# A two-layer encoder step on one core: the down-projection of the two middle feed-forwards by seven products with accumulation by DMA, other weights split in halves, six double places instead of five

## The chip, the cores and the metric

The kernel runs on one core of a Trainium2 chip. The metric is the device time of one execution in microseconds (us). Three executions of the kernel before took 2642.04, 2642.61 and 2645.54 us; the median is 2642.61 us. Everything read from a profile comes from one more execution, which took 2645.79 us.

## What is computed

A step of a hybrid encoder for 640 tokens (512 of a new stream and 8 times 16 of running streams) of width 1024. There are six sub-layers: feed-forward 0, mixer 0, feed-forward 1, feed-forward 2, mixer 1, feed-forward 3. The four feed-forwards are alike; cut to what matters:

```python
D_MODEL, D_FF = 1024, 2816

def swiglu(x, w_gate, w_up, w_down):
    return (jax.nn.silu(x @ w_gate) * (x @ w_up)) @ w_down

# around every feed-forward
x = layer_norm(ALPHA * x + 0.5 * swiglu(x, w_gate, w_up, w_down), g, b)
```

All arrays are float32. The change touches the last product, h @ w_down with h of 640 x 2816, in feed-forwards 1 and 2.

## The kernel before, in words

**Precision.** A product of float32 arrays is made of three matmuls. `split` (L92) writes a rounded high part with a cast on ScalarE (L93) and the rest, the low part, with a subtraction on VectorE (L94). A product then adds high x high, low x high and high x low in one PSUM bank. Every weight thus passes through ScalarE and VectorE before TensorE can use it: a DMA on SyncE's queue brings 128 x 1024 numbers to a `raw` place (four of them), and `split2` (L105) writes them as high and low parts to a double place `w` (a pool of `PAIRS` = 5, L29 and L46). A half, 128 x 512, goes to the single place `w1`.

**A feed-forward** (`ffn`) works through 22 blocks of 128 hidden channels. Blocks 0 and 1 are done plainly; the others in pairs f, f+1 by `pair` (L382). A pair needs two matrices, gate and up, and each of them is computed by the seven products of a 2 x 2 scheme in the place of eight. `operands` (L318) loads two weight blocks and prepares four operands: `u`, split from the raw weights, serves products 1 and 2; `v`, split from two sums, serves products 6 and 5; `w`, split from two differences, serves 7 and 3; the single `w1` serves 4. The two sums stand in the tile `sw` (L336, one buffer), s1 = a21 + a22 and s2 = s1 - a11, and are read again by the differences. `matrix` (L357) runs the products in the order 1, 2, 6, 5, 7, 3, 4, each of 12 matmuls with 320 columns, in three PSUM banks; it copies intermediate results to `mx` (ScalarE) and adds them to the results as they become ready (`take`). The gate's results pass through Silu, the up's are multiplied by it in `hf`, a float32 row of 640 tokens (two buffers), and `finish` (L243) splits that row to the high and low parts `h`.

**The down-projection** (`down`, L423) follows after four blocks: it loads four blocks of `w_down` and, for each of the five token tiles t and the two column halves j, adds 12 matmuls with 512 columns in a bank (`tm_proj`, L199), which VectorE scales and adds to the accumulator `yacc` (L206). That is 120 matmuls. It stands between the gate and the up matrix of the next group's first pair. A group of four blocks is so: gate, down of the group before, up, gate, up. Each feed-forward has five groups; the last one is projected at its end, together with the layer norm.

**Order.** A scheduler sets the order of the instructions of each engine when the program is built. On the chip each engine runs its list in that order and waits where an operand or a buffer is not ready.

Of the kernel before, what the change touches and what calls it, by code (L numbers as in the profile page):

```python
# [17 lines left out]
ALPHA = 4.0 ** 0.25  # L18
# [3 lines left out]
T = 640  # L22
TP = 512
NT = 5
KT = 8
NF = 22
HALVES = ((0, 256), (256, 384))
RAWS = 4
PAIRS = 5  # L29
PHASES = ("ffn0", "mix0", "ffn1", "ffn2", "mix1", "ffn3")  # L30
LN_OF = {"ffn0": 0, "mix0": 1, "ffn1": 2, "ffn2": 3, "mix1": 4, "ffn3": 5}

# [2 lines left out]
def kernel(ctx: ExitStack, tc: tile.TileContext, I, O, phases=PHASES):  # L35
    nc = tc.nc

    def pool(name, bufs=1, stack=ctx, **kw):
        return stack.enter_context(tc.tile_pool(name=name, bufs=bufs, **kw))
# [5 lines left out]

    pools = {"raw": pool("raw", RAWS), "w": pool("w", PAIRS), "w1": pool("w1", 1)}  # L46

# [28 lines left out]
    state = {"silu": None, "preload": None}  # L76
# [15 lines left out]
    def split(hi, lo, src):  # L92
        nc.scalar.copy(hi, src)  # L93
        return nc.vector.tensor_tensor(lo, src, hi.bitcast(F32), op=ALU.subtract)  # L94

    def raw_tile():
        return pools["raw"].tile([128, 1024], F32, name="raw")
# [4 lines left out]
    def two_units():  # L102
        return pools["w"].tile([128, 2, 2, 512], F32R, name="w")

    def split2(w, src):  # L105

        return split(w[:, :, 0], w[:, :, 1], src.rearrange("p (j c) -> p j c", j=2))

    def load_w(src):

        r = raw_tile()
        nc.sync.dma_start(r, src)
        w = two_units()
        split2(w, r)
        return w[:, 0], w[:, 1]

    def w_k(w, k):
# [8 lines left out]
    def mm3(ps, lhs, rhs):  # L126
        n = 3 * len(lhs)
        k = 0
        for (wh, wl), (xh, xl) in zip(lhs, rhs):
            for a, b in ((wh, xh), (wl, xh), (wh, xl)):  # L130
                state["pe"] = nc.tensor.matmul(ps, a, b, start=(k == 0), stop=(k == n - 1)).ins  # L131
                k += 1
# [3 lines left out]
    yacc = act.tile([128, NT, D], F32, name="yacc")  # L136
# [72 lines left out]
    def ffn(i, ph, last, side=None):  # L209


        V = nc.vector
        Q = T // 2
        with ExitStack() as st:
            wk = pool(f"ffn{i}_wk", 1, st, reuse_waits="tile")
            steps = side(wk) if side is not None else iter(())

            def tick(where):

                if ph == "ffn0" and where in range(NT):  # L220
# [40 lines left out]
            for h in range(2):  # L261
                o, L = HALVES[h]
# [86 lines left out]
            def product(ps, A, p, first):  # L349
                n = 0  # L350
                for k in range(4):
                    for a, b in ((0, 0), (1, 0), (0, 1)):
                        nc.tensor.matmul(ps, A[p][:, a, k * 128:k * 128 + 128], B[p][b][:, k, :],  # L353
                                         start=(first and n == 0), stop=(n == 11), skip_group_check=True)
                        n += 1

            def matrix(A, take):  # L357

                x, w, z = (bank_a()[:, :Q] for _ in range(3))
                e = {}  # L360

                def keep(n, ps):
                    e[n] = wk.tile([128, Q], F32, name="mx", bufs=3)
                    nc.scalar.copy(e[n], ps)  # L364


# [12 lines left out]
                product(x, A, 4, False)  # L379
                take(1, 0, x, None)  # L380

            def pair(f, before=None):  # L382
                g = first if f == 2 else {}

                def gate(r, c, ps, e):
                    if r not in g:
                        g[r] = g_row()
                    t = g[r][:, Q * c:Q * c + Q]
                    if e is not None:
                        V.tensor_tensor(t, ps, e, op=ALU.add)  # L390
                        ps = t
                    state["silu"] = nc.scalar.activation(t, ps, AF.Silu).ins

                def up(r, c, ps, e):
                    c = slice(Q * c, Q * c + Q)
                    t = row(f + r)
                    if e is not None:
                        V.tensor_tensor(t[:, c], ps, e, op=ALU.add)
                        ps = t[:, c]
                    if r == 0:  # L400
                        if c.start:
                            V.tensor_tensor(t, t, g[0], op=ALU.mult)
                            finish(f)
                    else:
                        V.tensor_tensor(t[:, c], ps, g[1][:, c], op=ALU.mult)
                        if not c.start:
                            finish(f + 1)

                for n, take in (("w_gate", gate), ("w_up", up)):
                    if n == "w_gate" and f == 2:  # L410
                        tick("gate")
                        continue
                    if n == "w_up" and before is not None:
                        down(before)
                    with tc.issue_after(state["acc0"]) if f == 2 else ExitStack():
                        A = operands(I[n][i, f], I[n][i, f + 1])
                    if n == "w_up":
                        for r in range(2):
                            ht[f + r] = h_tile()
                    matrix(A, take)  # L420
                    tick("gate" if n == "w_gate" else "up")

            def down(fs, norm=None):  # L423
                for f in fs:
                    wd[f] = load_w(I["w_down"][i, f])
                if norm is not None:
                    g_bc = [wk.tile([128, 2, 4, Q], F32, name=f"T{n}", bufs=1).rearrange("p a k c -> p (a k c)")[:, :D]
                            for n in (1, 2)]
                    load_gb(norm, g_bc)
                for t in range(NT):  # L430
                    tm_proj(t, [ht[f] for f in fs], [wd[f] for f in fs], 0.5 / ALPHA)
                    if t == 0 and fs[0] == 0:
                        state["acc0"] = state["acc"]
                        with tc.issue_after(state["acc"]):
                            t3_split()
# [1135 lines left out]
```

## Time and profile before

| what | number |
|---|---|
| median of three runs | 2642.61 us (2642.04 to 2645.54) |
| profiled execution | 2645.79 us |
| its span, first to last instruction | 2644.1 us |
| granted TensorE clock, mean over the span | 0.987 |
| busy: PE, VectorE (DVE), ScalarE (ACT), GpSimd (POOL) | 2559.6, 1914.1, 1118.3, 248.8 us |
| matmuls with 512 columns in the down-projections, of all four feed-forwards | 2640 |
| splits of a weight on DVE and of `sw` on DVE | 423 and 76 |
| HBM traffic over the span | 113 GB/s |

The profile names the engines PE (matmuls), PEld (weight loads, beside PE), DVE, ACT, POOL, and SPq for the DMAs that SyncE issues. A row of instructions says the line of the code, the engine, the operation and output <- inputs; then how many, the busy time and the mean duration of one, and the idle time of the engine before them with what ended it. Matmuls overlap one another: the mean duration of one is longer than the distance between two, so the distance is taken from the busy time of the group or from start times. Feed-forward 1 lies from about 780 to 1180 us, feed-forward 2 from there to about 1570 us.

### The profile page before, as it was taken

How to read it: one execution, taken by the hardware profiler on the slowest of the kernel's cores; microseconds unless marked ns; L12 is line 12 of the kernel's file. 1: busy time of each engine (PE TensorE's matmuls, PEld its weight loads, DVE VectorE, ACT ScalarE, POOL GpSimd, SP SyncE). 2: the span in 40 equal slices, each digit the busy share in tenths (PEclk: the TensorE clock that was granted, in tenths of full speed). 3: DMA queues.
4: the chain of work that ended last, by engine and by line, in shares of the span. 5: the costliest groups of instructions: out<-in, count | busy, mean ns of one | idle time of the engine just before them, and what ended most of it. 6: DMA issues, size and time to landing. Idle time of an engine off the chain costs nothing. (4 is left out here: it accounts for less than half of the span.)

```text
span 2644.1 us, 40071 instructions
## 1 busy us (share of the span) xinstructions
PE 2559.6 (97%) x15673; PEld 2315.7 (88%) x15673; DVE 1914.1 (72%) x3380; ACT 1118.3 (42%) x2050; POOL 248.8 (9%) x356
## 2 busy tenths in 40 slices
PE   8999999999879999999999999999999999999998
PEld 8999999887559999999999999988888878998887
DVE  7787777667858677657866567777675689876668
ACT  4433444346524344333433334566554444442332
POOL 0000002110021000003000002311121141000001
PEclk9999999999979999999999999999999999999999
DMA  5232334542312223222122223466463622443442
GB/s 178 96 99 88 103 109 144 181 144 77 93 44 71 81 96 96 70 82 98 64 76 85 87 80 106 124 183 208 123 199 111 230 90 86 159 141 109 139 129 98
DMA packets 165742, 302.72 MB, mean 114 GB/s; under 512 B 19072, under 2 KB 89856, under 8 KB 165040
## 3 DMA queue, kind: packets, MB, share of 16 engines
q1 hardware_dynamic: 163792, 293.83, 34.5%
q0 software_dynamic: 1760, 6.33, 0.7%
q8 instruction: 123, 2.02, 0.3%
q14 instruction: 67, 0.55, 0.1%
HBM read 259.56 MB, written 40.54 MB: 113 GB/s over the span
## 5 line engine op out<-in xcount | busy, mean ns | idle before, releaser
L131 PE MATMUL bank<-w,h 128*128 128x512 f32 x2640 | 612.1, 392 | 2.3 <-DVE w L94 2.3
L131 PEld LDWEIGHTS bank<-w,h 128*128 128x128 f32 x2640 | 493.5, 188 | 107.9 <-issue 3.4
L131 PE MATMUL bank<-xhi,w 128*128 128x256 f32 (+2 forms) x2528 | 560.7, 313 | 20.3 <-ACT w L93 14.2
L94 DVE TENSOR_TENSOR w<-raw,w 128x1024 fp32r<-128x1024 f32 (+1 forms) x423 | 476.4, 1136 | 121.5 <-ACT w L93 120.1
L353 PE MATMUL bank<-xhi,w 128*128 128x320 f32 x2432 | 539.6, 310 | 0.0
L93 ACT CAST w<-raw 128x1024 fp32r<-128x1024 f32 (+1 forms) x423 | 401.5, 970 | 180.0 <-DVE raw L332 81.6
L131 PEld LDWEIGHTS bank<-xhi,w 128*128 128x128 f32 x2528 | 424.0, 189 | 35.3 <-ACT w L93 15.6
L353 PE MATMUL bank<-T,w 128*128 128x320 f32 x2736 | 427.9, 310 | 3.5 <-ACT w L93 2.6
L353 PEld LDWEIGHTS bank<-T,w 128*128 128x128 f32 x2736 | 408.1, 188 | 5.3 <-ACT w L93 2.8
L353 PEld LDWEIGHTS bank<-xhi,w 128*128 128x128 f32 x2432 | 406.6, 188 | 5.5 <-issue 3.9
L131 PE MATMUL bank<-xlo,w 128*128 128x256 f32 (+2 forms) x1264 | 391.9, 311 | 1.2 <-DVE xlo L94 1.2
L353 PE MATMUL bank<-xlo,w 128*128 128x320 f32 x1216 | 375.5, 309 | 0.0
L206 DVE SCALAR_TENSOR_TENSOR yacc<-bank,yacc 128x512 f32<-128x512 f32 x240 | 164.8, 688 | 222.5 <-PE bank L131 222.4
L93 ACT CAST w<-sw 128x1024 fp32r<-128x1024 f32 x76 | 79.8, 1050 | 399.1 <-PE bank L131 270.3
L131 PEld LDWEIGHTS bank<-xlo,w 128*128 128x128 f32 x1264 | 239.5, 190 | 3.5 <-DVE xlo L94 1.7
L353 PEld LDWEIGHTS bank<-xlo,w 128*128 128x128 f32 x1216 | 228.2, 188 | 0.5 <-issue 0.5
L364 ACT COPY mx<-bank 128x320 f32<-128x320 f32 x228 | 96.6, 423 | 174.7 <-PE bank L353 174.2
L94 DVE TENSOR_TENSOR w<-sw,w 128x1024 fp32r<-128x1024 f32 x76 | 93.0, 1224 | 62.2 <-ACT w L93 61.8
L155 POOL DMA_DIRECT2D T<-in_ln_gb_dram x8 | 4.5, 568 | 1204.7 <-PE bank L353 796.5
L131 PE MATMUL bank<-w,og 128*128 128x512 f32 x432 | 106.6, 399 | 2.5 <-ACT og L1364 2.0
L131 PEld LDWEIGHTS bank<-w,og 128*128 128x128 f32 x432 | 81.0, 191 | 20.8 <-DVE og L1365 2.7
L1141 DVE SCALAR_TENSOR_TENSOR acc<-ext,cw,acc 128x512 f32<-128x512 f32 (+1 forms) x144 | 68.9, 546 | 29.8 <-POOL cvo L1131 16.7
(398 smaller groups left out, 2826.5 us busy)
## 6 DMA issues: line engine op xcount, KB each, us to landing
raw<-in_w_gate_dram SPq DMA_DIRECT2D x88, 512.0 KB, 4.1
raw<-in_w_up_dram SPq DMA_DIRECT2D x88, 512.0 KB, 4.3
raw<-in_w_down_dram SPq DMA_DIRECT2D x88, 512.0 KB, 4.1
raw<-in_m_in_dram SPq DMA_DIRECT2D x52, 512.0 KB, 4.3
raw<-in_m_out_dram SPq DMA_DIRECT2D x24, 512.0 KB, 4.1
csb<-cs_d SPq DMA_DIRECT2D x20, 512.0 KB, 5.5
h<-in_ssd_h_dram SPq DMA_DIRECT2D x16, 512.0 KB, 6.2
h<-in_ssd_h_dram SPq DMA_DIRECT2D x32, 256.0 KB, 2.8
```

The source lines that it names most:

```text
L93: nc.scalar.copy(hi, src)
L94: return nc.vector.tensor_tensor(lo, src, hi.bitcast(F32), op=ALU.subtract)
L131: state["pe"] = nc.tensor.matmul(ps, a, b, start=(k == 0), stop=(k == n - 1)).ins
L155: nc.gpsimd.dma_start(g_bc[j], bass.AP(tensor=I["ln_gb"].tensor, offset=I["ln_gb"].offset + (2 * n + j) * D, ap=[[0, 128], [1, D]]))
L206: state["acc"] = nc.vector.scalar_tensor_tensor(ya, pb, scale, ya, op0=ALU.mult, op1=ALU.add).ins
L353: nc.tensor.matmul(ps, A[p][:, a, k * 128:k * 128 + 128], B[p][b][:, k, :], start=(first and n == 0), stop=(n == 11), skip_group_check=True)
L364: nc.scalar.copy(e[n], ps)
L1141: V.scalar_tensor_tensor(o_, i_, cw[:, m, w:w + 1], o_, op0=ALU.mult, op1=ALU.add)
```

## The change

**Seven products in the down-projection.** In feed-forwards 1 and 2, `down` hands four of the five groups to the new `down7`: eight calls in all. Token tile 4 is done as before (24 matmuls). For the other four tiles, the tokens (two tiles of 128 each), the blocks (f and f+1) and the columns (two halves) make 2 x 2 blocks, and seven products of 6 matmuls stand in the place of eight, for two token pairs `tp`: 84 matmuls with 512 columns in the place of 96. The right operands are the four raw weight blocks, split to `direct`, and four combinations of them, made in place by eight VectorE operations (L459 to L462 of the new file) and split to `T`: eight double places in the place of four. The left operands are `h` itself and sums of it: `row_sums`, called at the end of every up matrix of such a group, makes four sums of 128 x 256 in an `sw` tile (the same single buffer that `operands` uses) and splits them to `hs`.

**Accumulation by DMA.** Each of the 14 results of `down7` is copied by ScalarE from PSUM to `ev` (128 x 512, three buffers) and added to `yacc` by a DMA that GpSimd issues (`accum_op`): 112 DMAs of 256 KB. The banks of token pair 0 and 1 are used again by later products.

**Other weights.** `load_w`, used for all weights outside `operands` and `down7`, splits each half of 512 columns by itself. `PAIRS` is 6. The memory kept for the descriptors of GpSimd's DMAs is set to 4096 bytes of a partition.

The core of the diff:

```diff
-PAIRS = 5
+PAIRS = 6
+SEVEN = ("ffn1", "ffn2")
...
         w = two_units()
-        split2(w, r)
+        for j in range(2):
+            split(w[:, j, 0], w[:, j, 1], r[:, 512 * j:512 * j + 512])
...
                     matrix(A, take)
+                    if n == "w_up" and ph in SEVEN and f < NF - 4:
+                        row_sums(f)
...
+            def row_sums(f):
+                v = wk.tile([128, 1024], F32, name="sw", bufs=1)
+                s1, s2, s3, s4 = (v[:, 256 * n:256 * n + 256].rearrange("p (n c) -> p n c", n=2) for n in range(4))
+                p, q = by_pairs(hf[f]), by_pairs(hf[f + 1])
+                V.tensor_tensor(s1, p[:, :, 1], q[:, :, 1], op=ALU.add)
+                V.tensor_tensor(s2, s1, p[:, :, 0], op=ALU.subtract)
+                V.tensor_tensor(s3, p[:, :, 0], p[:, :, 1], op=ALU.subtract)
+                V.tensor_tensor(s4, q[:, :, 0], s2, op=ALU.subtract)
+                o = hs[f] = wk.tile([128, 2, 1024], F32R, name="hs", bufs=2)
+                split(o[:, 0], o[:, 1], v)
...
+                def product(ps, tp, p, first):
+                    n = 0
+                    for f in fs[::2]:
+                        a, b = left(f, p, tp), right(f, p)
+                        for u, v in ((0, 0), (1, 0), (0, 1)):
+                            nc.tensor.matmul(ps, a[:, u], b[:, v], start=(first and n == 0), stop=(n == 5),
+                                             skip_group_check=True)
+                            n += 1
+                def add(ps, t, j):
+                    e = wk.tile([128, 512], F32, name="ev", bufs=3)
+                    nc.scalar.mul(e, ps, 0.5 / ALPHA)
+                    nc.gpsimd.dma_start(yacc[:, t, 512 * j:512 * j + 512], e, accum_op=ALU.add)
...
+                x, w = ([bank_b() for _ in range(2)] for _ in range(2))
+                z = [bank_a() for _ in range(2)]
+                for p, ps, a, j in ((1, x, 0, 0), (2, z, 0, 0), (5, w, 1, 1), (6, x, 0, 1), (3, w, 0, 1), (7, x, 1, 1),
+                                    (4, x, 1, 0)):
+                    for tp in range(2):
+                        product(ps[tp], tp, p, p in (1, 2, 5))
+                        add(ps[tp], 2 * tp + a, j)
...
             def down(fs, norm=None):
+                if ph in SEVEN and len(fs) == 4 and norm is None:
+                    return down7(fs)
...
+    nc = _bacc.Bacc("TRN2", target_bir_lowering=False, num_devices=1, dynamic_dma_scratch_size=4096)
```

**How the instructions move.** The first place is the end of an up matrix in feed-forward 1, where the next gate matrix begins. On DVE before (L314-L340 are `operands`, L398 to L405 the up's results, `w_9026` is `v` of the next gate, made from `sw_9028`; `h` are the two finished rows):

```order
L332 TENSOR_TENSOR sw_9028<-sw_9028,raw_9021 128x512
L94 TENSOR_TENSOR w_9026<-sw_9028,w_9026 128x2x512
L332 TENSOR_TENSOR raw_9021<-raw_9021,sw_9028 128x512
L332 TENSOR_TENSOR raw_9021<-raw_9021,raw_9022 128x512
L398 TENSOR_TENSOR hf_8987<-bank_8916,mx_8973 128x320
L405 TENSOR_TENSOR hf_8987<-hf_8987,s_8863 128x320
L94 TENSOR_TENSOR w_9027<-raw_9021,w_9027 128x2x512
L398 TENSOR_TENSOR hf_8945<-bank_8917,mx_8959 128x320
L94 TENSOR_TENSOR w_9146<-raw_9144,w_9146 128x2x512
L402 TENSOR_TENSOR hf_8945<-hf_8945,s_8820 128x640
L405 TENSOR_TENSOR hf_8987<-bank_8916,s_8863 128x320
```

The next gate's `v` and `w` (`w_9027`) are split before the up's last result is taken (the last row).

At the same place on DVE now (lines are two higher than before; `w_9222` is `v` of the next gate, made from `sw_9224`; `sw_9209` holds the row sums, L439 to L442, and `hs_9214` is their split; L392 takes the gate's second product):

```order
L407 TENSOR_TENSOR hf_9175<-bank_9104,s_9051 128x320
L95 TENSOR_TENSOR h_9102<-hf_9133,h_9102 128x640
L439 TENSOR_TENSOR sw_9209<-hf_9133,hf_9175 128x256
L95 TENSOR_TENSOR w1_9235<-raw_9218,w1_9235 128x512
L95 TENSOR_TENSOR h_9103<-hf_9175,h_9103 128x640
L440 TENSOR_TENSOR sw_9209<-sw_9209,hf_9133 128x256
L442 TENSOR_TENSOR sw_9209<-hf_9175,sw_9209 128x256
L392 TENSOR_TENSOR s_9267<-bank_9240,mx_9253 128x320
L95 TENSOR_TENSOR hs_9214<-sw_9209,hs_9214 128x1024
L334 TENSOR_TENSOR sw_9224<-raw_9218 128x512
L334 TENSOR_TENSOR sw_9224<-sw_9224,raw_9217 128x512
L95 TENSOR_TENSOR w_9222<-sw_9224,w_9222 128x2x512
```

The up's last result is now the first row, and `v` the last one, behind the row sums, their split and the gate's second product. The rows stand in this order at all 16 ends of an up matrix that have row sums.

On PE before, the end of the gate's product 2 (bank_9044) and its products 6 and 5, which read `v`:

```order
L353 MATMUL bank_9044<-xlo_83,w_9025 128x320
L353 MATMUL bank_9044<-xhi_82,w_9025 128x320 x2
L353 MATMUL bank_9044<-xlo_83,w_9025 128x320
L353 MATMUL bank_9042<-T2_7802,w_9026 128x320 x12
L353 MATMUL bank_9043<-T1_7801,w_9026 128x320 x12
```

On PE now, the same products:

```order
L355 MATMUL bank_9240<-xlo_83,w_9221 128x320
L355 MATMUL bank_9240<-xhi_82,w_9221 128x320 x2
L355 MATMUL bank_9240<-xlo_83,w_9221 128x320
L355 MATMUL bank_9238<-T2_7922,w_9222 128x320
L355 MATMUL bank_9239<-T1_7921,w_9222 128x320
L355 MATMUL bank_9238<-T2_7922,w_9222 128x320 x11
L355 MATMUL bank_9239<-T1_7921,w_9222 128x320 x11
```

Nothing has come between products 2 and 6; only the first matmul of product 5 stands ahead of the second of product 6.

The second place is `down7` on ACT (`ev` are the copies out of PSUM, in the order of the products; the casts are high parts of `T`, then of the next up matrix):

```order
L492 ACTIVATE ev_9420<-bank_9408 128x512
L94 CAST w_9374<-raw_9342 128x2x512
L94 CAST w_9377<-raw_9346 128x2x512
L492 ACTIVATE ev_9429<-bank_9409 128x512
L492 ACTIVATE ev_9438<-bank_9412 128x512
L94 CAST w1_9558<-raw_9541 128x512
L492 ACTIVATE ev_9447<-bank_9413 128x512
L492 ACTIVATE ev_9456<-bank_9410 128x512
L492 ACTIVATE ev_9465<-bank_9411 128x512
L492 ACTIVATE ev_9474<-bank_9408 128x512
L94 CAST w_9544<-raw_9540 128x2x512
L492 ACTIVATE ev_9483<-bank_9409 128x512
```

Two casts stand between the first and the second copy, and one before the eighth. On POOL the DMAs of the same call, with their waits (DMASW is an earlier DMA of POOL, Activation the copy):

```order
L493 DMA yacc_84<-ev_9420 128x512 [waits Activation_49]
L493 DMA yacc_84<-ev_9429 128x512 [waits Activation_49]
L493 DMA yacc_84<-ev_9438 128x512 [waits DMASW5_49,DMASW3_49,Activation_49]
L493 DMA yacc_84<-ev_9447 128x512 [waits DMASW6_49,DMASW4_49,Activation_49]
L493 DMA yacc_84<-ev_9456 128x512 [waits DMASW7_49,Activation_49]
```

The third and the fourth DMA add to the same rows of `yacc` as the first and the second, and wait for them to land.

More of the change, by code (lines that the diff above doesn't have):

```diff
@@ L420, in pair, with by_pairs @@
                     matrix(A, take)
+                    if n == "w_up" and ph in SEVEN and f < NF - 4:
+                        row_sums(f)
                     tick("gate" if n == "w_gate" else "up")
+            def by_pairs(t):
+                return t[:, :TP].rearrange("p (n a c) -> p n a c", n=2, a=2)
+            hs = {}
+            def row_sums(f):
[8 more added lines that the diff above has]
+                split(o[:, 0], o[:, 1], v)
@@ new lines, in down7, with left, right @@
+            def down7(fs):
+                raws, direct = {}, {}
+                for f in fs:
+                    raws[f] = raw_tile()
+                    nc.sync.dma_start(raws[f], I["w_down"][i, f])
+                for f in fs:
+                    direct[f] = two_units()
+                    split2(direct[f], raws[f])
+                for f in fs[::2]:
+                    (b11, b12), (b21, b22) = ((r[:, :512], r[:, 512:]) for r in (raws[f], raws[f + 1]))
+                    V.tensor_tensor(b22, b22, b12, op=ALU.subtract)
+                    V.tensor_tensor(b12, b12, b11, op=ALU.subtract)
+                    V.tensor_tensor(b11, b22, b11, op=ALU.add)
+                    V.tensor_tensor(b21, b21, b11, op=ALU.subtract)
+                T = {}
+                for r in range(2):
+                    for f in fs[::2]:
+                        T[f + r] = two_units()
+                        split2(T[f + r], raws[f + r])
+                def left(f, p, tp):
+                    tok = lambda k, a: ht[f + k][:, :, 256 * tp + 128 * a:256 * tp + 128 * a + 128]
+                    if p in (1, 2, 4):
+                        return tok(*{1: (0, 0), 2: (1, 0), 4: (1, 1)}[p])
+                    o = 256 * {5: 0, 6: 1, 7: 2, 3: 3}[p] + 128 * tp
+                    return hs[f][:, :, o:o + 128]
+                def right(f, p):
+                    return {1: direct[f][:, 0], 2: direct[f + 1][:, 0], 3: direct[f + 1][:, 1],
+                            6: T[f][:, 0], 5: T[f][:, 1], 4: T[f + 1][:, 0], 7: T[f + 1][:, 1]}[p]
+                def product(ps, tp, p, first):
+                    n = 0
+                    for f in fs[::2]:
+                        a, b = left(f, p, tp), right(f, p)
[7 more added lines that the diff above has]
+                    nc.gpsimd.dma_start(yacc[:, t, 512 * j:512 * j + 512], e, accum_op=ALU.add)
+                t = NT - 1
+                for j in range(2):
+                    pb = bank_a()
+                    mm3(pb, [(ht[f][:, 0, t * 128:t * 128 + 128], ht[f][:, 1, t * 128:t * 128 + 128]) for f in fs],
+                        [(direct[f][:, j, 0], direct[f][:, j, 1]) for f in fs])
+                    ya = yacc[:, t, j * 512:j * 512 + 512]
+                    state["acc"] = V.scalar_tensor_tensor(ya, pb, 0.5 / ALPHA, ya, op0=ALU.mult, op1=ALU.add).ins
+                x, w = ([bank_b() for _ in range(2)] for _ in range(2))
[5 more added lines that the diff above has]
+                        add(ps[tp], 2 * tp + a, j)
@@ L1538 @@
     lay = _layout(inputs)
-    nc = _bacc.Bacc("TRN2", target_bir_lowering=False, num_devices=1)
+    nc = _bacc.Bacc("TRN2", target_bir_lowering=False, num_devices=1, dynamic_dma_scratch_size=4096)
     arrays, I, O = {}, {}, {}
```

## The prediction

> **What bounds the kernel now.** I read the page first, then the stretch of feed-forwards 1 and 2 by windows, PE's waits, the groups by form, and at last the timeline around one end of an up matrix.
>
> ```profile
> PE 2559.6 (97%) x15673; PEld 2315.7 (88%) x15673; DVE 1914.1 (72%) x3380; ACT 1118.3 (42%) x2050; POOL 248.8 (9%) x356
> 800.00:1600.00 800.00, 799.10 (x4802) 751.05 (x4800) 551.59 (x827) 307.06 (x480) 25.56 (x20) 1.00 0.25 82
> PE bank L131 <- ACT w L93: 14.2, 5, 6.3
> PE bank L353 <- ACT w L93: 2.6, 1, 2.6
> ```
>
> PE is busy for 97% of the span, and in the window that holds both changed feed-forwards for 799.10 of 800 us at a granted clock of 1.00. There, PE alone sets the time: DVE works 69% of it, ACT 38%, both just ahead of PE. A matmul less is time less there, and a wait put in front of PE is time more, with no slack to take it up. In the whole kernel PE waits for split weights little (the two waits named are 16.8 us together).
>
> **What is saved.** The distance of two matmuls is busy time over count:
>
> ```profile
> L131 PE MATMUL bank<-w,h 128*128 128x512 f32 x2640 | 612.1, 392 | 2.3 <-DVE w L94 2.3
> ```
>
> 612.1 / 2640 = 0.232 us for 512 columns. A call of `down7` has 24 + 84 = 108 matmuls in place of 120; 12 less, in 8 calls, are 96 x 0.232 = **22.3 us less**. All of it lies on PE's path.
>
> **The wait for the row sums.** What else is moved must be laid beside the old timeline at the end of an up matrix:
>
> ```profile
> 939.76 1.19 PE L353 MATMUL bank<-T,w 128*128 128x320 f32 x7
> 940.70 0.82 DVE L402 TENSOR_TENSOR hf<-hf,s 128x640 f32<-128x640 f32 x1
> 940.79 0.46 PE L353 MATMUL bank<-xhi,w 128*128 128x320 f32 x2
> 941.43 0.48 DVE L405 TENSOR_TENSOR hf<-bank,s 128x320 f32<-128x320 f32 x1
> 943.10 1.55 DVE L94 TENSOR_TENSOR h<-hf,h 128x640 fp32r<-128x640 f32 x2
> 944.30 3.68 PE L353 MATMUL bank<-T,w 128*128 128x320 f32 x24
> 944.57 0.68 DVE L94 TENSOR_TENSOR w<-raw,w 128x512 fp32r<-128x512 f32 x1
> 946.70 0.68 DVE L332 TENSOR_TENSOR sw<-raw 128x512 f32<-128x512 f32 x1
> 947.42 0.69 DVE L332 TENSOR_TENSOR sw<-sw,raw 128x512 f32<-128x512 f32 x1
> 947.68 0.33 PEld L353 LDWEIGHTS bank<-xhi,w 128*128 128x128 f32 x2
> 948.34 1.05 ACT L93 CAST w<-sw 128x1024 fp32r<-128x1024 f32 x1
> 949.43 1.22 DVE L94 TENSOR_TENSOR w<-sw,w 128x1024 fp32r<-128x1024 f32 x1 [1.32 <-ACT w L93]
> ```
>
> Call T the moment at which PE leaves the up matrix (here 940.79). Products 1 and 2 of the gate take 944.30 - 940.79 = 3.51 us (24 matmuls, 0.147 each); then PE wants `v`. Before, `v` had been split ahead of T, by the order of the first place in the section on the change. Now `v` comes from an `sw` tile that is free only when the row sums in it are split, and these need the up's last result. So a chain starts at T that PE waits for. By these rows, in DVE's new order: the result is there at about T + 0.3 (the old row ran at T + 0.6, behind L402); L407 0.48, split of h 0.78 (half of 1.55), a row sum 0.42 (estimate: rows of 320 and 640 elements take 0.48 and 0.82, so some 1.0 ns an element), the single's low part 0.68, the other h 0.78, two row sums 0.84: T + 4.3. Then 0.2 to reach ACT (the gap 948.11 to 948.34), the cast of `hs` 1.05, its low part 1.22, the two sums 0.68 and 0.69, a gap of 0.2, the cast of `v` 1.05, its low part 1.22, about 0.2 to PE: T + 10.8. PE reached `v` at T + 3.5, and in between has only the two matmuls that need the high part alone (0.3). It waits 10.8 - 3.8 = **7.0 us**. L392, which takes product 2, can start at T + 3.8 and hides behind the cast of `hs`.
>
> A lower bound holds whatever the row sums take. In DVE's order L392 stands ahead of the rest, and it needs product 2: from there 0.2 for the hand-over, 0.48 (L392, as L405), 1.22 (low part of `hs`), 1.37 (two sums), 0.2, 1.05 and 1.22 (`v`), 0.2 are 5.9; less 0.3, 5.6 us. The upper one is 7.5, with 0.05 more at each of some ten hand-overs. No work of another kind covers it: PE's list has nothing between. The order has this at all 16 ends: 16 x 7.0 = **112 us more** (90 to 120).
>
> **The clock after the wait.** The trace of before has such waits in mixer 0:
>
> ```profile
> 722.64 0.40 PE L131 MATMUL bank<-w,xhi 128*128 128x512 f32 x1
> 729.18 1.54 PE L882 MATMUL bank<-ident,S 128*128 128x128 f32 x6 [6.14 <-ACT S L81]
> 724.00:726.00 2.00, 0.00 (x0) 0.00 (x0) 2.00 (x3) 1.33 (x2) 0.00 (x0) 0.77 0.78 233
> 726.00:728.00 2.00, 0.00 (x0) 0.00 (x0) 2.00 (x3) 1.23 (x2) 0.00 (x0) 0.50 0.07 29
> 762.29 0.78 PE L131 MATMUL bank<-w,xhi 128*128 128x512 f32 x1
> 764.00:766.00 2.00, 2.00 (x6) 1.52 (x6) 0.82 (x1) 0.14 (x1) 0.00 (x0) 0.50 0.00 0
> 766.00:768.00 2.00, 2.00 (x10) 1.65 (x9) 0.90 (x2) 0.00 (x0) 0.00 (x0) 0.99 0.00 0
> ```
>
> PE stops at 723.04 and the granted clock is 0.50 from about 725 on. Dense matmuls begin again at 762.29 and run 6 in 2 us until about 766.0, then 10. So after a wait of 6 us some 3.7 us of work go at half speed and 1.9 us are lost: 16 x 1.9 = **30 us more**; bounds 0 (the clock stays) and, for twice that stretch, 60. Later small waits in the gate (product 7 needs a low part that is ready about 0.5 us late by the same chain) vanish behind the slow stretch; I price them at nothing, and at 16 x 0.5 = 8 us without it. The Trainium skill, "TensorE: Matmul & The Clock Gate", Part 1, says that the activity window is some 3.4 us long and free-running, so that a slow stretch lasts one to two windows; by that the term would be an estimated 27 to 54 us, and the trace's 3.7 us is at its short end.
>
> **The results by DMA.** Before, DVE took a result straight to `yacc`; now ACT copies it and a DMA adds it, and three `ev` buffers hold PE back if the DMA is slow. No accumulating DMA is in the trace of before. The nearest rows:
>
> ```profile
> T<-in_ln_gb_dram POOLq DMA_DIRECT2D x8, 512.0 KB, 6.0
> raw<-in_w_down_dram SPq DMA_DIRECT2D x88, 512.0 KB, 4.1
> h<-in_ssd_h_dram SPq DMA_DIRECT2D x32, 256.0 KB, 2.8
> out_ssd_s_dram<-h SPq DMA_DIRECT2D x32, 256.0 KB, 2.1
> L93 ACT CAST xhi<-bank 128x512 fp32r<-128x512 f32 x50 | 27.0, 584 | 17.2 <-PE bank L193 17.2
> L93 ACT CAST w<-raw 128x1024 fp32r<-128x1024 f32 x346 | 356.6, 1050 | 135.5 <-DVE raw L332 81.6 <-PE bank L353 16.9 <-issue 9.4
> ```
>
> A transfer of 512 KB lands 1.9 us later from POOL than from SP; 256 KB by SP take 2.1 to 2.8, on the mean 2.4; so I take **4.3 us** from issue to landing, between 2.1 and 6.0. A product of `down7` is 6 x 0.232 = 1.39 us, a copy 0.6. At 4.3 the longest chain, from the start of the first product: the second copy stands behind two casts (2.1 us) and ends at 4.9; its DMA lands at 9.2; the fourth DMA, to the same rows, waits for it and lands at 13.6; the seventh copy, which needs that buffer, ends at 14.3; a cast (1.05) and the eighth copy, 16.0; its DMA lands at 20.3; the eleventh copy ends at 21.0; and product 13, which adds in that bank, starts at 21.2 where it would have at 12 x 1.39 = 16.7. Product 14 waits 1.4 us more in the same way: in all 5.9 us a call, **47 us more** in 8. At 2.8 us the chain is just hidden (0), at 6.0 it costs 12.7 a call, 102 us. The Trainium skill, "DMA: Bandwidth & Descriptors", Anatomy of one DMA, gives a DMA from GpSimd about 2.0 us and the bytes at 436 GB/s: an estimated 2.6 us here, by which this term is 0. For 512 KB it would be 3.2, and the trace has 6.0; I go by the trace.
>
> **Edits at nothing.**
>
> ```profile
> L206 DVE SCALAR_TENSOR_TENSOR yacc<-bank,yacc 128x512 f32<-128x512 f32 x240 | 164.8, 688 | 222.5 <-PE bank L131 222.4
> L93 ACT CAST w<-raw 128x512 fp32r<-128x512 f32 x76 | 46.9, 616 | 44.5 <-PE bank L353 29.4 <-DMA raw<-in_w_up_dram 12.6 <-issue 2.3
> ```
>
> A call gives DVE 8 combinations (5.5 us), 4 more splits (4.9) and two sets of row sums (5.8), and takes 8 results of L206 away (5.5): some 11 us more beside PE's 70 to 80 a group. DVE has 31% of the window free, and all of this but the chain above is queued ahead of its use, so I price it at nothing; without that cover it would cost what DVE's work exceeds PE's. The halves cost ACT 2 x 0.62 - 1.05 = 0.2 us a weight beside PE, and give the first half 0.4 us sooner; the sixth place allows earlier loads. At best both take half of the 16.8 us of waits quoted at the start, in sub-layers where the order also changes: 0, with 8 us either way.
>
> **The sum**, against the profiled execution's 2645.8: -22.3 + 112 + 30 + 47 = +166.7, so 2812.5; the median of the runs shown is 3.2 us below that execution, so **2809 us**.
>
> **Rivals.**
> - The DMA lands within 2.8 us (for it: the SP rows; against: POOL's 6.0). Then PE never waits for a bank: 2809 - 47 = 2762. Chance 0.25; the DMA page's rule gives the same.
> - The DMA takes 6.0 or more, with the second read and the weights' traffic beside it (for it: POOL's row; against: half the bytes): 2809 + 55 = 2864. Chance 0.13.
> - The clock is not lowered by these waits (for it: two matmuls interrupt them; against: in mixer 0 it fell 2 us after PE had stopped): 2809 - 30 + 8 = 2787. Chance 0.07.
> - Faster: the chain from T to the low part of `v` is as short as PE's cover, 3.5 us, at which point only the 22.3 us are left: 2642.6 - 22.3 = 2620. It speaks for it that DVE and ACT have idle time; against it that the low part of `hs`, the two sums and `v`'s two parts alone are 1.22 + 1.37 + 1.05 + 1.22 = 4.9 us of measured durations in a row. Chance 0.03.
>
> **How the numbers follow.** The forecast as summed has 0.51; a chance of 0.01 is left for gains and losses that cancel. A measurement of this kernel tells about 0.2% (5 us) from no change: faster 0.03, same 0.01, slower 0.96. The range goes from the quick DMA with waits of 6 us (2762 - 16) to the slow one with the upper bound of the waits and 8 us elsewhere (2864 + 8 + 8): 2745 to 2880.
>
> **What would show it.** Right: PE idle in front of L355 about 7 us, 16 times, put down to DVE or ACT `w`; a granted clock that dips to 0.5 behind each; waits of L485 for ACT `ev`, and `ev` for a DMA, of some 6 us a call; DMAs of L493 landing after about 4.3 us; matmuls with 512 columns down by 96. Wrong: waits under 5.6 us at the 16 ends (the order's bound is misread), a clock of 1.00 through them, no wait at L485, or a loss outside feed-forwards 1 and 2.

## The result, and the profile after

The changed kernel takes **2808.19 us** (median of 4 runs, 2805.84 to 2810.18), the one before 2642.32 us on the same chip (4 runs, 2641.3 to 2645.54): a ratio of 1.0625, 95% interval 1.0607 to 1.0644. The forecast was 2809 us. The time is right to 1 us by luck: two of its terms are wrong by over 20 us, in opposite directions. The intervals of the runs below reach some 3 to 6 us to each side, so that differences of a few us between runs are not told apart.

The page after: the first rows are the busy times, the last the additions to `yacc`.

```profile
span 2805.4 us, 40790 instructions
PE 2597.0 (93%) x15577; PEld 2335.0 (83%) x15577; DVE 2021.5 (72%) x3654; ACT 1247.7 (44%) x2372; POOL 336.5 (12%) x468
...
PEclk9999999999799999999999999999999999999999
...
yacc<-ev POOLq DMA_DIRECT2D x112, 256.0 KB, 4.5
```

There are 96 matmuls less (15577 for 15673), and yet PE is busy for 37.4 us more and idle for 123.9 us more (208.4 for 84.5; idle is span less busy). The clock of each fortieth hardly shows it. Feed-forwards 1 and 2 do, by windows that end with the last statistics of each layer norm (the order of columns: PE, PEld, DVE, ACT and POOL busy, granted clock, share of the DMA engines, GB/s):

```profile
793.10:1322.40 529.30, 456.64 (x2540) 418.21 (x2540) 345.40 (x520) 226.44 (x352) 71.53 (x76) 0.92 0.38 96
1322.40:1847.10 524.70, 454.01 (x2521) 414.37 (x2521) 345.66 (x521) 226.48 (x353) 71.37 (x75) 0.93 0.38 97
1847.10:2353.10 506.00, 494.94 (x3249) 444.44 (x3248) 389.09 (x864) 285.07 (x778) 107.22 (x200) 1.00 0.53 165
```

By the same marks they were, before:

```profile
800.50:1231.40 430.90, 430.24 (x2586) 403.53 (x2585) 299.61 (x452) 168.54 (x261) 24.02 (x20) 1.00 0.26 84
1231.40:1662.30 430.90, 427.81 (x2562) 401.02 (x2561) 299.79 (x453) 167.47 (x261) 23.98 (x19) 1.00 0.26 84
```

Each of the two was 430.9 us long and is now 529.3 and 524.7; PE is idle for 14% of them and the clock is 0.92 and 0.93. (The section on the time before put them too early. The window from 800 to 1600 us, which the prediction read, lies inside them but for its first 0.5 us, and ends 62 us before the second one does.) The third row of the first view is mixer 1, which the prediction left as it was; it is 24.2 us shorter.

PE's waits over the whole kernel, in total, number and longest, lead with three that were not there:

```profile
PE bank L355 <- ACT w L94: 82.2, 16, 5.2
PE bank L485 <- ACT ev L492: 46.2, 26, 3.0
PE bank L355 <- DVE w L95: 6.0, 17, 0.4
```

The first and third are the 16 ends of an up matrix, the second the calls of `down7`. The timeline of one such end, with T = 961.86, PE's first matmul of the gate:

```profile
961.86 0.46 PE L355 MATMUL bank<-xhi,w 128*128 128x320 f32 x2
962.06 0.49 DVE L407 TENSOR_TENSOR hf<-bank,s 128x320 f32<-128x320 f32 x1
965.33 0.43 DVE L442 TENSOR_TENSOR sw<-hf,sw 128x256 f32<-128x256 f32 x1
965.67 0.48 DVE L392 TENSOR_TENSOR s<-bank,mx 128x320 f32<-128x320 f32 x1
965.79 1.04 ACT L94 CAST hs<-sw 128x1024 fp32r<-128x1024 f32 x1 [1.49 <-DVE sw L442]
966.87 1.23 DVE L95 TENSOR_TENSOR hs<-sw,hs 128x1024 fp32r<-128x1024 f32 x1 [0.71 <-ACT hs L94]
968.13 0.69 DVE L334 TENSOR_TENSOR sw<-raw 128x512 f32<-128x512 f32 x1
968.85 0.69 DVE L334 TENSOR_TENSOR sw<-sw,raw 128x512 f32<-128x512 f32 x1
969.58 1.04 ACT L94 CAST w<-sw 128x1024 fp32r<-128x1024 f32 x1 [2.37 <-DVE sw L334]
970.65 1.23 DVE L95 TENSOR_TENSOR w<-sw,w 128x1024 fp32r<-128x1024 f32 x1 [1.11 <-ACT w L94]
970.67 0.90 PE L355 MATMUL bank<-T,w 128*128 128x320 f32 x2 [5.13 <-ACT w L94]
971.93 5.16 PE L355 MATMUL bank<-T,w 128*128 128x320 f32 x22 [0.36 <-DVE w L95]
```

Read it as one chain: the row sums end at T + 3.9, their split at T + 6.2, the two sums for `v` at T + 7.7, its low part at T + 10.0, and PE goes on at T + 10.07. The 22 matmuls take 5.16 us where 24 took 3.68 before. The same stretch by windows shows why:

```profile
966.00:968.00 2.00, 0.00 (x0) 0.00 (x0) 1.29 (x2) 1.21 (x2) 0.00 (x0) 1.00 0.00 0
968.00:970.00 2.00, 0.00 (x0) 0.00 (x0) 1.48 (x3) 0.42 (x1) 0.00 (x0) 0.70 0.00 0
972.00:974.00 2.00, 2.00 (x8) 2.00 (x9) 1.08 (x2) 0.88 (x1) 0.00 (x0) 0.50 0.00 0
974.00:976.00 2.00, 2.00 (x10) 2.00 (x10) 1.80 (x2) 1.54 (x3) 0.00 (x0) 0.59 0.79 242
976.00:978.00 2.00, 2.00 (x16) 2.00 (x15) 1.85 (x3) 0.51 (x2) 0.00 (x0) 1.00 0.67 215
```

Here the clock falls some 3 us after PE has stopped, and returns some 5 us after it has begun again: 8 matmuls in 2 us, then 16. By the trace it falls to 0.50 at all 16 places, 2.0 to 5.3 us after the stop, and is back at 1.00 3.7 to 7.0 us after PE has begun again.

The second new wait, in the first call of `down7` (PE, ACT and POOL rows of the timeline):

```profile
1026.05 0.86 POOL L493 DMA_DIRECT2D yacc<-ev  x1 [1.77 <-ACT ev L492]
1026.41 5.60 PE L485 MATMUL bank<-w,hs 128*128 128x512 f32 x24
1033.53 0.60 ACT L492 ACTIVATE ev<-bank 128x512 f32<-128x512 f32 x1 [4.71 <-DMA yacc<-ev]
1034.18 3.01 PE L485 MATMUL bank<-w,hs 128*128 128x512 f32 x12 [2.16 <-ACT ev L492]
1044.21 4.45 PE L485 MATMUL bank<-w,h 128*128 128x512 f32 x12 [2.63 <-ACT ev L492]
```

And three stretches of it by windows:

```profile
1026.00:1032.00 6.00, 6.00 (x27) 4.66 (x25) 1.40 (x2) 1.46 (x3) 1.72 (x2) 1.00 1.00 234
1044.00:1046.00 2.00, 1.79 (x4) 1.49 (x5) 1.86 (x3) 0.47 (x2) 1.73 (x2) 0.50 0.93 161
1046.00:1048.00 2.00, 2.00 (x7) 1.55 (x6) 0.76 (x1) 1.78 (x4) 0.86 (x1) 0.67 1.01 173
```

The second addition is issued at 1026.05, and then the DMA engines are fully busy (share 1.00, 234 GB/s: weights come in beside it). The fifth copy, which needs its buffer, starts at 1033.53: 7.5 us later, where 4.3 was assumed. Over the 112 additions the time to landing runs from 3.3 to 8.0 us, with the median at 4.5. That the weights' traffic makes the late ones late is likely and was not tested by a run of its own. PE stands for it at its ninth product. And the clock falls in the call as well (0.50 from 1044): the last 12 matmuls take 4.45 us, where 12 took 3.01 at full clock.

### The profile page after: what moved, and what is told of

Same layout as the page of the kernel before. It is cut to its first block, busy times and chain, and to the rows that moved or that the text cites. A ratio compares the mean times of both kernels' runs of the same rounds, so it can differ in the third digit from the quotient of the medians.

```text
span 2805.4 us, 40790 instructions
## 1 busy us (share of the span) xinstructions
PE 2597.0 (93%) x15577; PEld 2335.0 (83%) x15577; DVE 2021.5 (72%) x3654; ACT 1247.7 (44%) x2372; POOL 336.5 (12%) x468
## 5 line engine op out<-in xcount | busy, mean ns | idle before, releaser
L95 DVE TENSOR_TENSOR w<-raw,w 128x512 fp32r<-128x512 f32 (+1 forms) x617 | 539.0, 896 | 238.5 <-ACT w L94 236.2
L94 ACT CAST w<-raw 128x512 fp32r<-128x512 f32 (+1 forms) x617 | 453.1, 771 | 312.3 <-PE bank L133 114.4
L355 PE MATMUL bank<-T,w 128*128 128x320 f32 x2736 | 467.1, 327 | 90.2 <-ACT w L94 82.2
L133 PE MATMUL bank<-w,h 128*128 128x512 f32 x1872 | 436.7, 391 | 0.7 <-DVE w L95 0.7
L133 PEld LDWEIGHTS bank<-w,h 128*128 128x128 f32 x1872 | 348.1, 188 | 76.3 <-issue 3.4
L493 POOL DMA_DIRECT2D yacc<-ev x112 | 97.1, 911 | 810.4 <-ACT ev L492 501.4
L208 DVE SCALAR_TENSOR_TENSOR yacc<-bank,yacc 128x512 f32<-128x512 f32 x160 | 109.6, 687 | 80.0 <-PE bank L133 79.2
L400 DVE TENSOR_TENSOR hf<-bank,mx 128x320 f32<-128x320 f32 x120 | 58.6, 488 | 106.0 <-PE bank L355 100.7
L492 ACT ACTIVATE ev<-bank 128x512 f32<-128x512 f32 x112 | 65.9, 596 | 129.7 <-DMA yacc<-ev 103.3
L485 PE MATMUL bank<-w,hs 128*128 128x512 f32 x384 | 96.3, 403 | 22.1 <-ACT ev L492 22.1
```

The costliest lines, as they stand in the source:

```text
L208: state["acc"] = nc.vector.scalar_tensor_tensor(ya, pb, scale, ya, op0=ALU.mult, op1=ALU.add).ins
L485: nc.tensor.matmul(ps, a[:, u], b[:, v], start=(first and n == 0), stop=(n == 5), skip_group_check=True)
L492: nc.scalar.mul(e, ps, 0.5 / ALPHA)
L493: nc.gpsimd.dma_start(yacc[:, t, 512 * j:512 * j + 512], e, accum_op=ALU.add)
```

## The experiments

The theory after the result: PE's path in the two feed-forwards carries two separate additions, the chain through the single `sw` tile and the copies with their DMAs, each with its wait and the slower clock behind it; the seven products themselves pay. The rival: the waits are one and the same shortage (DVE or ACT), so that taking one away only shows the other. All ten runs, each against the kernel before on the same chip, with PE's busy and idle time of each profiled execution:

| run | median us | ratio to before, 95% interval | span | PE busy | PE idle |
|---|---|---|---|---|---|
| before | 2642.32 | 1 | 2644.1 | 2559.6 | 84.5 |
| after | 2808.19 | 1.0625 (1.0607 to 1.0644) | 2805.4 | 2597.0 | 208.4 |
| row sums in tiles of their own | 2675.81 | 1.0127 (1.0112 to 1.0142) | 2676.3 | 2556.9 | 119.4 |
| results added by DVE | 2738.47 | 1.0373 (1.0353 to 1.0393) | 2736.3 | 2574.6 | 161.7 |
| both | 2607.21 | 0.9868 (0.9854 to 0.9883) | 2606.4 | 2531.0 | 75.4 |
| matmuls that fill the wait | 2787.51 | 1.0552 (1.0537 to 1.0568) | 2787.5 | 2652.4 | 135.1 |
| no seven products | 2622.90 | 0.9922 (0.9907 to 0.9937) | 2623.3 | 2552.2 | 71.1 |
| six places alone | 2627.11 | 0.9932 (0.9911 to 0.9954) | 2625.0 | 2552.4 | 72.6 |
| halves alone | 2637.41 | 0.9980 (0.9971 to 0.9990) | 2635.8 | 2557.2 | 78.6 |
| four buffers for copies | 2791.69 | 1.0557 (1.0539 to 1.0574) | 2790.4 | 2594.2 | 196.2 |
| less memory for descriptors | 2809.30 | 1.0622 (1.0606 to 1.0639) | 2807.4 | 2601.1 | 206.3 |
| plain writes, no addition | 2762.07 | 1.0441 (1.0417 to 1.0465) | 2760.4 | 2584.4 | 176.0 |

### Row sums in tiles of their own

```diff
-                v = wk.tile([128, 1024], F32, name="sw", bufs=1)
+                va, vb = (wk.tile([128, 512], F32, name="ev", bufs=3) for _ in range(2))
...
-                split(o[:, 0], o[:, 1], v)
+                split(o[:, 0, :512], o[:, 1, :512], va)
+                split(o[:, 0, 512:], o[:, 1, 512:], vb)
```

> The row sums stand in two tiles of their own (of the three that the copies out of PSUM use) and no longer in sw; all else as in the changed kernel. Theory A (the 16 waits in the gate matrix, with the slow clock behind them, come from the one sw tile): each gate matrix behind row sums goes back from some 20.5 to 12.2 us, about 2808 - 16 x 8.4 = 2674 us, and the 16 waits of PE for ACT w are gone. Rival B (the work of the row sums itself on DVE and ACT delays v, wherever they stand): little change, 2790 us or more, waits still there.

2675.81 us: theory A. The 16 waits for `w` are gone from the list of PE's waits, the ones for copies are as they were:

```profile
PE bank L486 <- ACT ev L493: 45.6, 25, 3.0
```

The changed kernel less this one is 129.1 us of span: 89.0 idle and 40.1 busy. The chain through the single tile, with the clock behind it, costs that. (The split of the sums in two halves came with the two tiles and was not tried apart; but `v` of the next gate is split before the up's last result again, as in the kernel before, so that the chain as a whole is gone.)

### Results added by DVE

```diff
-                    e = wk.tile([128, 512], F32, name="ev", bufs=3)
-                    nc.scalar.mul(e, ps, 0.5 / ALPHA)
-                    nc.gpsimd.dma_start(yacc[:, t, 512 * j:512 * j + 512], e, accum_op=ALU.add)
+                    ya = yacc[:, t, 512 * j:512 * j + 512]
+                    state["acc"] = V.scalar_tensor_tensor(ya, ps, 0.5 / ALPHA, ya, op0=ALU.mult, op1=ALU.add).ins
```

> The 14 results of each call go straight from PSUM to yacc by VectorE, as in the kernel before, with no copy and no DMA; the sums still stand in sw. Theory A (a call waits for ev and its DMAs, and the clock falls there too, some 9 us a call): 2808 - 8 x 9 = 2736 us, no wait for ev, a call near 25 us. Theory A with the prediction's size (5.9 us a call): 2761 us. Rival B (VectorE, with 112 more operations of 0.69 us, becomes late for the splits and gives it back): 2780 us or more, with new waits of PE for DVE.

2738.47 us: theory A with 9 us a call. The 16 waits of the same 82.2 us remain, and none for `ev`. The DMA path costs 69.1 us of span: 46.7 idle and 22.4 busy.

### Both

> Both edits of the two runs before together. Theory A (the two are separate stretches and add up): about 2808 - 134 - 72 = 2602 us, faster than the kernel before, granted clock back near 0.99. Rival B (each cover hides the other's cost, or VectorE is the next bound): 2640 us or more.

2607.21 us: the fastest of all, 1.3% under the kernel before. The two edits together take 199.0 us off the span, singly 129.1 and 69.1. They add up to 1 us, so the rival falls: the waits are two causes, not one shortage. DVE, with the additions back, is not the bound.

### No seven products

```diff
-SEVEN = ("ffn1", "ffn2")
+SEVEN = ()
```

> The changed kernel with down7 and row_sums never called: the halves, the sixth double place and the small descriptor memory alone. Theory A (the 31 us that the sub-layers outside feed-forwards 1 and 2 became shorter come from these): 2642 - 31 = 2611 us, with feed-forwards 1 and 2 at the old 431 us each. Rival B (they come from the scheduler's other order behind the changed feed-forwards): 2635 to 2645 us.

2622.90 us, between the two expectations: what is left (halves, six places, descriptors' memory) is 19.4 us faster than before. By windows with the marks used above, mixer 1 takes 506.0 us, as in the changed kernel, so that its gain comes from these edits; but feed-forward 1 takes 437.9 us and not the old 431, and the cause of that stays open. Against it the run with both edits shows what 96 matmuls are worth when nothing waits for them: busy 2531.0 for 2552.2, 21.2 us less; span 16.9 less.

### Six places alone, halves alone

```diff
-PAIRS = 5
+PAIRS = 6
...
+    nc = _bacc.Bacc("TRN2", target_bir_lowering=False, num_devices=1, dynamic_dma_scratch_size=4096)
```

> The kernel before with six double places and the small descriptor memory; weights split whole. Theory A (the gain outside is the sixth place, which lets weights be split earlier in mixer 1): 2615 to 2620 us. Rival B (it is the halves): 2640 us, as before.

```diff
-        split2(w, r)
+        for j in range(2):
+            split(w[:, j, 0], w[:, j, 1], r[:, 512 * j:512 * j + 512])
```

> The kernel before with the weights of load_w split in halves; five places, the old descriptor memory. Theory A (the sixth place): 2640 us, as before. Rival B (the halves give the first matmuls of a weight 0.4 us sooner, some 190 times): 2612 to 2620 us.

2627.11 and 2637.41 us: the first lies between its two expectations, the second is 3 us below its theory A. (The run with six places has the smaller memory for descriptors with them.) The places carry the larger part of the gain, and it lies in mixer 1: the whole of it, and one stretch, before

```profile
1662.30:2192.50 530.20, 504.45 (x3237) 448.96 (x3236) 379.85 (x808) 279.29 (x722) 110.98 (x200) 0.98 0.51 158
1982.00:2022.00 40.00, 33.47 (x200) 29.64 (x199) 21.76 (x48) 19.28 (x58) 4.18 (x10) 0.87 0.28 84
```

and with six places

```profile
1663.80:2173.40 509.60, 498.11 (x3238) 444.84 (x3237) 385.35 (x809) 278.93 (x722) 109.87 (x200) 0.99 0.53 164
1984.00:2024.00 40.00, 40.00 (x269) 36.45 (x268) 26.79 (x54) 20.49 (x60) 5.91 (x10) 1.00 0.40 125
```

Mixer 1 is 20.6 us shorter with the same matmuls: 14.3 of it PE's idle time, 6.3 busy time. In the second row of before lies a wait of 4.49 us for a split weight, with the clock down to 0.87; with six places PE has no idle time there. Halves alone shorten mixer 1 by 6.8 us. The three edits together gain less than the parts added (20.8 us of span for 19.1 and 8.3): presumably both remove the same waits.

### Matmuls that fill the wait

```diff
+                if fill:
+                    d = bank_b()[:, :Q]
+                    for _ in range(fill):
+                        nc.tensor.matmul(d, A[1][:, 0, :128], B[1][0][:, 0, :], start=True, stop=True)
```

In the changed kernel, 36 matmuls between products 2 and 6 at the 16 gate matrices; nobody reads their bank.

> As the changed kernel, with 36 idle matmuls (product 1's operands into a spare bank that nobody reads) between products 2 and 6 of the gate matrix, at the 16 places with row sums: 5.3 us of PE work inside a wait of 6.3 us. It computes the same results. Theory A (the slow matmuls behind the wait come from the clock that falls in it): the clock stays at 1.00 there, about 2.3 us a place are won, 2808 - 37 = 2771 us. Rival B (they are slow because VectorE and ScalarE are late with the next parts): 2808 us, the 36 matmuls only fill the wait.

```profile
962.42 0.45 PE L355 MATMUL bank<-xhi,w 128*128 128x320 f32 x2
965.94 5.44 PE L375 MATMUL bank<-xhi,w 128*128 128x320 f32 x36
970.14 1.05 ACT L94 CAST w<-sw 128x1024 fp32r<-128x1024 f32 x1 [2.37 <-DVE sw L334]
971.24 0.56 PE L355 MATMUL bank<-T,w 128*128 128x320 f32 x2
972.50 3.49 PE L355 MATMUL bank<-T,w 128*128 128x320 f32 x22 [0.70 <-DVE w L95]
```

That is the gate of the timeline above (the first row is its first matmul, T = 962.42 here), and here by windows:

```profile
970.00:972.00 2.00, 1.80 (x12) 1.41 (x10) 0.88 (x2) 1.05 (x1) 0.00 (x0) 1.00 0.00 0
972.00:974.00 2.00, 1.50 (x10) 1.50 (x11) 1.65 (x3) 0.32 (x1) 0.00 (x0) 1.00 0.00 0
```

2787.51 us, between the two expectations. With work in the wait the clock stays at 1.00, at all 16 places by the trace, and the 22 matmuls take 3.49 us in place of 5.16. Over the kernel, the row of the matmuls with `T` on the page was, in the changed kernel and with the wait filled:

```profile
L355 PE MATMUL bank<-T,w 128*128 128x320 f32 x2736 | 467.1, 327 | 90.2 <-ACT w L94 82.2
L355 PE MATMUL bank<-T,w 128*128 128x320 f32 x2736 | 432.0, 310 | 12.6 <-DVE w L95 11.2
```

So 35.1 us of busy time hang on the clock that falls in the idle stretch: that the slow stretch comes from the idle PE is so shown. The filling costs nothing here: PE goes on with the two matmuls at T + 8.82 and with the 22 at T + 10.08, where it did at T + 8.81 and T + 10.07 without it, because the cast of `v` ends as late as before. Why the run brought 20.7 us and not 37: the faster PE is sooner at its next waits. The two matmuls take 0.56 in place of 0.90 us, and the wait for the low part behind them grows by as much (11.4 us in all, from 6.0). From its first matmul to the first one behind it a gate matrix shortens by 1.7 us (18.9 in place of 20.5 on the mean of the 16, by the trace), 27 us in all. The waits for copies grew to 52.1 from 46.2 us, and why was not tested.

### Four buffers for copies

```diff
-                    e = wk.tile([128, 512], F32, name="ev", bufs=3)
+                    e = wk.tile([128, 512], F32, name="ev", bufs=4)
...
-    nc = _bacc.Bacc("TRN2", target_bir_lowering=False, num_devices=1, dynamic_dma_scratch_size=4096)
+    nc = _bacc.Bacc("TRN2", target_bir_lowering=False, num_devices=1, dynamic_dma_scratch_size=2048)
```

> The changed kernel with four buffers for the copies in place of three; the room comes from 2048 bytes less for the descriptors of GpSimd's DMAs. In the changed kernel PE waits 46.2 us for copies, and the copies wait 103.3 us for an earlier accumulation to land; in the first call the fifth copy waits 4.71 us, because the second accumulation lands only some 7 us after its issue. Theory A (three buffers are what lets a late landing through to PE; with four the fifth copy hangs on the first accumulation, which has landed): PE's waits for copies fall to some 25 us, PE's busy time falls by 10 us with the clock that no longer falls in the call, and the kernel takes 2765 to 2790 us. Theory B (the waits are set by the rate at which the accumulations land, and by the order in which two results of the same rows must land): a fourth buffer moves the waits a little, and the time stays within 8 us of 2808.

The second edit alone is the measure for it:

> The changed kernel with 2048 bytes in place of 4096 for the descriptors of GpSimd's DMAs and nothing else, as the measure beside the run with four buffers. Theory A (the memory for descriptors is never full): 2808 us, within 5, and the same median of the landings, 4.5 us. Theory B (a smaller memory makes GpSimd wait before it can write descriptors): an issue takes longer than 0.86 us or waits, and the kernel is over 8 us slower.

2791.69 and 2809.30 us. Halving the descriptors' memory costs nothing. The fourth buffer brings 17.6 us: 2 us short of theory A's range, and more than theory B allowed. With four, PE's waits for copies are

```profile
PE bank L485 <- ACT ev L492: 35.9, 23, 2.8
```

and the additions, by the view of L493, land after

```profile
DMA to landing us min/median/max: 3.3/5.6/9.5
```

One more DMA is under way, and each lands later, 5.6 us for 4.5. A fourth buffer takes away a quarter of the cost; what the landing has to do with the rest is tried next.

### Plain writes in place of additions

```diff
-                    nc.gpsimd.dma_start(yacc[:, t, 512 * j:512 * j + 512], e, accum_op=ALU.add)
+                    nc.gpsimd.dma_start(yacc[:, t, 512 * j:512 * j + 512], e)
```

> The changed kernel with the 112 DMAs of the results as plain writes to the accumulator in place of additions (the sum in the accumulator is thereby left out: each result replaces what stood there). All instructions, queues and waits stay. It tells what of the DMA path's 70.8 us hangs on the addition. Theory A (the addition makes the transfer slow, since it reads and writes the accumulator, and 112 transfers take 6.0% of 16 engines' span for 29 MB, where SyncE's queue takes 32.9% for 294 MB): the landing falls from 4.5 to 2.5 to 3.5 us, PE's waits for copies from 46 to below 20 us, and the kernel takes 2740 to 2770 us. Theory B (the issue by GpSimd and the queueing behind other transfers set the landing): it stays at 4 us or more, and the kernel within 10 us of 2808.

2762.07 us: theory A. (What the expectation calls 70.8 us is 69.1 by spans, 69.7 by medians.) An issue by GpSimd, from the timeline:

```profile
1026.34 0.54 POOL L493 DMA_DIRECT2D yacc<-ev  x1 [2.09 <-DMA yacc<-ev]
```

The landing, by the view of L493:

```profile
DMA to landing us min/median/max: 2.2/2.5/6.1
```

PE's waits for copies:

```profile
PE bank L485 <- ACT ev L492: 17.6, 17, 2.0
```

GpSimd's queue on the page (packets, MB, share of 16 engines):

```profile
q0 software_dynamic: 10720, 35.69, 3.5%
```

The same row of the changed kernel, with additions:

```profile
q0 software_dynamic: 17888, 35.69, 6.7%
```

For the same bytes the addition takes 144 packets a transfer in place of 80 (the 1760 of before taken off, over 112), 0.86 us of GpSimd in place of 0.54, and lands 2.0 us later. It is 45.0 of the DMA path's 69.1 us of span; 24.1 are left with plain writes.

## Why the prediction was right, and where it was not

By spans, the way from before to after is: halves and places -20.8, the seven products without their waits -16.9, the two waits with their clock +199.0; together +161.3 (by the medians -19.4, -15.7 and +201.0, together 165.9). The prediction had 0, -22.3 and +189.

- **What bounds the kernel.** Right. Feed-forwards 1 and 2 became 192.2 us longer, of which 139.6 are idle time of PE and 52.6 busy time. Putting the 112 additions back on DVE made the kernel faster and lengthened none of PE's main waits for DVE: its work counts only where PE waits for it.
- **The saving, -22.3.** Right: 21.2 us of busy time. Of it 16.9 reach the span, since the run with both edits idles 4.3 us more than the one without seven products.
- **The wait for the row sums, 112.** The mechanism and its place are right, all 16 of them: a resume at T + 10.07 where T + 10.8 was worked out, no single step of the chain off by more than 0.4 us. PE's idle time in it is 89.0 us by the run with tiles of their own, under the bounds of 90 to 120; by the two rows of waits it is 5.5 us a place, just under the 5.6 that the prediction named as a sign that it had misread the order's bound. The bound was not misread: from the end of product 2 (T + 3.68) to the resume are 6.4 us. The two matmuls in between were put at 0.3 us; they take 0.90 at the lowered clock and count as busy. With 0.3 the wait would be 6.1 us, 98 in all.
- **The clock, 30.** Right in kind and near in size, shown by the filled wait. The busy time that goes with the row sums is 40.1 us, 2.5 a place where mixer 0 had suggested 1.9. The stretch of 3.7 us of slow work was read in mixer 0 from 762.29 us on, 33 us behind the wait of 6.14 us and after shorter waits, and was the shortest of what came (3.7 to 7.0). Of the 40.1, 35.1 go with the clock. The Trainium skill, "TensorE: Matmul & The Clock Gate", Part 1, by which the prediction estimated 27 to 54 us, agrees with it. The wait and the clock together are 129.1 where 142 was predicted.
- **The DMA, 47.** Mis-sized: 69.1. The step that failed is "in all 5.9 us a call" as the whole price. PE's idle time is as predicted, 46.2 us of waits, that is 5.8 a call. But it came from the ninth product on, not the thirteenth, as in the call shown the second addition took 7.5 us to land, beside the weights' traffic; and a slow clock was priced for the row sums alone, while these waits too bring 22.4 us of busy time, most of it slow clock: by the trace it falls to 0.50 in seven of the eight calls. Nor is the chain "just hidden" at 2.8 us: plain writes with a median of 2.5 (and a longest of 6.1) still cost 24.1.
- **"0, with 8 us either way" outside.** Failed: -20.8 by the run without seven products, with -24.2 in mixer 1 alone. The step held that halves and places could save at most half of the 16.8 us of waits for split weights. It counted the waits by their sum over the kernel and left out what a wait does to the clock behind it, the very thing that it priced elsewhere, and the other waits of mixer 1 (25.8 us of idle PE there, 11.5 with six places).

So the total is near by luck, because errors cancel: 22 us too little for the DMA against 21 us too much for the neutral edits, and 13 us too much at the row sums against a saving 5 us too large. The sign never hung on that; the match to 1 us did.

What stays open: why feed-forward 1 is 7 us longer in the run without seven products than before; which of mixer 1's waits the sixth place removes directly, and which through the changed order; and what the remaining 24.1 us of plain writes split into.

## What to carry to other kernels

Where one engine is busy for 97% and everything else runs just ahead of it, lay each new step on the old timeline at the point where that engine wants its next operand: a shared buffer with one copy set a loss of 129 us against a saving of 21. Price every new wait of TensorE with the slow clock behind it, short waits too, and price an edit that takes such waits away in the same way. And before a result is handed to an adding DMA, ask how long its buffer is held; here VectorE did the same work, and hardly a wait of TensorE came with it.

## What the runs showed of the hardware

- An addition by DMA costs about twice a plain write of the same 256 KB: 4.5 us to landing for 2.5, 6.0% of the 16 engines' time for 2.8% (the 0.7% of before taken off). The Trainium skill, "DMA: Bandwidth & Descriptors", Anatomy of one DMA, gives some 2.0 us and the bytes at 436 GB/s, an estimate of 2.6 us: the plain write agrees with it, the addition does not.
- Waits under 3 us can lower the clock. In the call shown it was still 1.00 after a PE wait of 2.16 us. After one of 2.63 us that came 10 us later, with waits of 0.79 and 0.27 in between, it stood at 0.50 and 0.67 for the next 4 us. The Trainium skill, "TensorE: Matmul & The Clock Gate", HAM oscillation, puts the rule as no idle gaps of TensorE over some 3.4 us; here gaps below that, several of them close together, went before the fall.
